# A sliding-window copy: staged batches stored as 127 rows a half instead of 128, with 15 of them on the software ring

## The chip, the cores and the metric

The kernel runs on one core of one Trainium2 chip. The metric is the device time of one execution in microseconds, the median of several; lower is better. There is no arithmetic: the kernel only moves bytes with DMAs. DMAs are issued on three queues, called rings here: SP's and ScalarE's (hardware descriptor generation; q1 and q10 in the profile) and GpSimd's (software; q0, POOL in the profile). All three feed the same 16 DMA engines.

## The reference

```python
def setup_inputs():
    batch, length, dim = (32, 4096, 256)
    window_size = 64
    stride = 32
    return {'x': np.random.randn(batch, length, dim).astype(np.float32), 'window_size': window_size, 'stride': stride}

def reference(x, window_size, stride):
    batch, length, dim = x.shape
    n_windows = (length - window_size) // stride + 1
    result = np.zeros((batch, n_windows, window_size, dim), dtype=np.float32)
    for i in range(n_windows):
        start = i * stride
        result[:, i] = x[:, start:start + window_size].copy()
    return result
```

A batch of `x` is 4096 rows of 256 float32, 4.19 MB. Cut into blocks of 32 rows it has 128 blocks of 32 KB. Window i is the blocks i and i + 1, so the 127 windows of a batch are 8.3 MB of output, in which every block but the first and the last stands twice: as the left half of window i and as the right half of window i - 1. The whole output is 266.3 MB.

## The kernel before, in words

Each batch takes one of two ways.

Twenty *direct* batches are copied from HBM to HBM. `Copier.windows` (L29, its DMA at L34) copies n windows, or n left or right halves. SP's ring copies 16 half windows (16 rows of 32 KB, 512 KB) with each DMA, 14 DMAs a batch, 280 in all (`blocks`, L166). The remaining 15 windows of a batch are one DMA of 960 KB on the software ring (`remainder`, L170); the last batch's 15 are spread over five DMAs there. That makes 24 DMAs on the software ring, all issued at the start.

Twelve *staged* batches go through SBUF on ScalarE's ring, in two groups of six tiles (`Staging`, L61). A tile `xb` has 128 rows, one block of 32 KB in each partition. `load` (L78) fills it (HBM is read once), and two half stores write it out: half 0 puts row p into the left half of window p, half 1 puts row p into the right half of window p - 1. A row is written 64 KB apart from the next, as two packets of 16 KB.

A half needs only 127 rows: row 127 is no left half, row 0 no right half. Before, all 128 rows are stored all the same, as one DMA of 128 rows or two of 64 (every other row). The row too many lands in the neighbouring batch: the left half of row 127 in window 0 of the batch after, the right half of row 0 in the last window of the batch before. So what belongs there has to be written later:

- where the neighbour is a direct batch, SP's DMA that writes that place is held back to the end (`spoilt`, L175) and waits until the staged batch is stored (`wait_stored`, L114);
- the last two staged batches are neighbours of each other; `store_pair` (L102) orders their stores, with a wait on `spilt` in the middle.

The order on each ring is written out by hand. ScalarE: six loads, twelve half stores, six loads (each waits until the tile's former batch is stored, L82), twelve half stores. GpSimd: the 24 remainders, then a drain. SP: one DMA, then three more that wait for remainders 7, 11 and 16 to land and all the rest after 17 (`back`, L192 to L198), then the held-back ones, then the waits for everything (L205).

Of the kernel before, what the change touches and what calls it, by code (L numbers as in the profile page):

```python
# [11 lines left out]
class Copier:  # L12


    def __init__(self, x, out, B, L, D, W, S, n_win):
        assert W == 2 * S and L % S == 0
        self.x, self.out = x, out
        self.B = B
        self.blk = S * D
        self.nb = L // S  # L20
        self.nw = n_win
# [18 lines left out]
    def load(self, q, t, b, c, rows):  # L40

        p, step, n, unit = rows
        return q.dma_start(
            out=t[p : p + (n - 1) * step + 1 : step, :],
            in_=self.xap(b * self.nb + c + p // unit, [[step // unit * self.blk, n], [1, self.blk]]),
            max_dma_last_dim=IN,
        )

    def store(self, q, t, b, c, rows, half):


        p, step, n, unit = rows
        w = b * self.nw + c + p // unit - half
        return q.dma_start(
            out=self.oap(2 * w + half, [[2 * step // unit * self.blk, n], [1, self.blk]]),
            in_=t[p : p + (n - 1) * step + 1 : step, :],
            max_dma_last_dim=OUT,
        )


class Staging:  # L61


    def __init__(self, c, tc, pool, dtype, items, bufs):
        self.c, self.items = c, items
        self.tiles = [pool.tile([128, c.blk], dtype, name=f"xb{i}") for i in range(bufs)]
        self.loaded = [tc.alloc_semaphore(f"loaded{i}") for i in range(bufs)]
        self.stored = [tc.alloc_semaphore(f"stored{i}") for i in range(bufs)]
        self.spilt = tc.alloc_semaphore("spilt")
        self.ended = tc.alloc_semaphore("ended")  # L70
        self.count = {sem: 0 for sem in (*self.loaded, *self.stored, self.spilt, self.ended)}
        self.after_load, self.after_store = {}, {}

    def issue(self, dma, sem):
        dma.then_inc(sem, 16)
        self.count[sem] += 16

    def load(self, q, g):  # L78
        i = g % len(self.tiles)
        b = self.items[g]  # L80
        if self.count[self.stored[i]]:
            q.wait_ge(self.stored[i], self.count[self.stored[i]])  # L82
        parts = [(k, 4, 32, 1) for k in range(4)] if g == 0 else [(0, 1, 128, 1)]
        for rows in parts:
            self.issue(self.c.load(q, self.tiles[i], b, 0, rows), self.loaded[i])
        self.after_load[g] = self.count[self.loaded[i]]

    def put(self, q, g, part, half, sem):
        k, n = part
        i = g % len(self.tiles)  # L90
        self.issue(self.c.store(q, self.tiles[i], self.items[g], 0, (k, n, 128 // n, 1), half), sem)

    def store(self, q, g):
        i = g % len(self.tiles)
        q.wait_ge(self.loaded[i], self.after_load[g])
        for half in (0, 1):
            n = 1 if (2 * g + half) % 4 == 3 else 2
            for k in range(n):
                self.put(q, g, (k, n), half, self.stored[i])
        self.after_store[g] = self.count[self.stored[i]]  # L100

    def store_pair(self, q, g):  # L102

        for k in (g, g + 1):
            q.wait_ge(self.loaded[k % len(self.tiles)], self.after_load[k])
        even, odd = (0, 2), (1, 2)
        for k, part, half in ((g, even, 1), (g, odd, 0), (g + 1, odd, 0), (g + 1, even, 1)):
            self.put(q, k, part, half, self.spilt)
        self.put(q, g, even, 0, self.ended)
        q.wait_ge(self.spilt, self.count[self.spilt])  # L110
        for k, part, half in ((g + 1, even, 0), (g, odd, 1), (g + 1, odd, 1)):
            self.put(q, k, part, half, self.ended)

    def wait_stored(self, q, g):  # L114

        if g in self.after_store:
            q.wait_ge(self.stored[g % len(self.tiles)], self.after_store[g])
        else:
            q.wait_ge(self.spilt, self.count[self.spilt])

    def run(self, q):
        bufs = len(self.tiles)
        for first in range(0, len(self.items), bufs):
            group = range(first, min(first + bufs, len(self.items)))
            for g in group:
                self.load(q, g)
            pair = group[-1] == len(self.items) - 1
            for g in group[:-2] if pair else group:
                self.store(q, g)
            if pair:  # L130
                self.store_pair(q, group[-2])


@with_exitstack
def kernel(
    ctx: ExitStack,
    tc: tile.TileContext,
    x: bass.AP,
    window_size: bass.AP,
    stride: bass.AP,  # L140
    out: bass.AP,
):
    nc = tc.nc
    W, S = int(window_size), int(stride)
    B, L, D = x.shape
    n_win = (L - W) // S + 1
    assert out.shape == (B, n_win, W, D)
    c = Copier(x, out, B, L, D, W, S, n_win)


    staged = [1, 4, 7, 10, 13, 16, 19, 22, 24, 26, B - 3, B - 2]
    place = {b: g for g, b in enumerate(staged)}
    direct = [b for b in range(B) if b not in staged]
    pool = ctx.enter_context(tc.tile_pool(name="xb", bufs=1))
    st = Staging(c, tc, pool, x.dtype, staged, 6)
    ring_d, ring_s, ring_r = nc.sync, nc.scalar, nc.gpsimd
    done = tc.alloc_semaphore("done")
    rest = tc.alloc_semaphore("rest")
    back = {i: tc.alloc_semaphore(f"back{i}") for i in (7, 11, 16, 17)}
    total = {done: 0, rest: 0, **dict.fromkeys(back.values(), 0)}  # L160

    def count(dma, sem):
        dma.then_inc(sem, 16)
        total[sem] += 16

    def blocks(part):  # L166
        for b, w, half in part:
            count(c.windows(ring_d, b, w, 16, half), done)

    def remainder(b, w, n, half=None, piece=DIRECT, sem=rest):  # L170
        count(c.windows(ring_r, b, w, n, half, piece), sem)

    first, last = 48, B - 1
    halves = [(b, w + (15 if w >= first else 0), half) for b in direct for w in range(0, 112, 16) for half in (0, 1)]
    spoilt = {(b + d, 0 if d > 0 else c.nw - 16, 0 if d > 0 else 1): g for b, g in place.items() for d in (1, -1) if b + d in direct}  # L175
    halves = [h for h in halves if h not in spoilt]
    spoilt = sorted(spoilt, key=spoilt.get)
    with tc.tile_critical():
        st.run(ring_s)

        pairs = iter([(first + d, half) for d in (0, 2) for half in (0, 1)])
        for i, b in enumerate(direct[:-1]):
            if i in (8, 9, 12, 13):
                w, half = next(pairs)
                remainder(last, w, 2, half, DIRECT // 2)
            if i == 4:
                remainder(last, first + 4, 11)
            remainder(b, first, 15, piece=DIRECT // 2 if i in (1, 3, 4, 15, 18) else DIRECT, sem=back.get(i, rest))
        ring_r.drain()  # L189

        blocks(halves[:1])
        ring_d.wait_ge(back[7], 16)  # L192
        blocks(halves[1:2])
        ring_d.wait_ge(back[11], 16)
        blocks(halves[2:3])
        ring_d.wait_ge(back[16], 16)
        blocks(halves[3:4])
        ring_d.wait_ge(back[17], 16)  # L198
        blocks(halves[4:])
        for h in spoilt:  # L200
            b = h[0] + (-1 if h[1] == 0 else 1)
            st.wait_stored(ring_d, place[b])
            blocks([h])
        total[st.ended] = st.count[st.ended]
        for sem, n in total.items():  # L205
            ring_d.wait_ge(sem, n)


# [33 lines left out]
```

## Time and profile before

| what | value |
|---|---|
| time, median of 3 runs | 748.22 us (747.45 to 749.07) |
| the profiled execution | 747.89 us |
| its span | 746.1 us |
| bytes moved by DMAs | 317.50 MB, mean 426 GB/s |
| ScalarE's ring (q10) | 151.00 MB |
| SP's ring (q1) | 146.82 MB |
| software ring (q0) | 19.66 MB |

Compute engines do nothing here but issue DMAs, so the parts of the profile on busy engines and on the chain of work say little. What carries the time is the row of DMA engines over the 40 slices of the span (digits are tenths of busy, the GB/s below), the table of queues (packets, MB, share of the sixteen engines' span), the waits of the issuing sequencers, and the list of DMA issues with the time from issue to landing. Beside these answers the trace holds a record of each packet (start, duration, size, queue; the engine is not named) and the times at which each DMA's sixteen completions landed; where a text says "the records", it is these.

### The profile page before, as it was taken

The numbers are of one execution on the slowest core, as the hardware profiler recorded it, in microseconds if no ns is written. First come the engines' busy times: TensorE is split into PE (matmuls) and PEld (weight loads), VectorE is DVE, ScalarE is ACT, GpSimd is POOL, SyncE is SP. The second block draws the span as 40 slices with busy tenths as digits, with TensorE's granted clock in tenths as the row PEclk, the third lists the DMA queues.
The fourth block names the chain that finished last, engine by engine and source line by source line (L and its number), as shares of the span: only waits on it lengthen the run. The fifth ranks groups of instructions, "written<-read, shape, count | busy, mean of one in ns | idle before, by whom it ended". The sixth has DMA issues, their size and how long they took to land. (4 is left out here: it accounts for less than half of the span.)

```text
span 746.1 us, 419 instructions
## 1 busy us (share of the span) xinstructions
POOL 14.0 (2%) x28
## 2 busy tenths in 40 slices
POOL 7000000000000000000000000000000000000000
DMA  8999999999999999999999999999999999999997
GB/s 364 433 419 430 441 416 428 428 432 429 431 432 432 434 427 433 432 432 429 432 406 432 433 432 429 432 426 433 430 428 432 433 428 431 430 432 435 430 430 326
DMA packets 20418, 317.50 MB, mean 426 GB/s; under 512 B 5962, under 2 KB 5962, under 8 KB 5962
## 3 DMA queue, kind: packets, MB, share of 16 engines
q10 hardware_dynamic: 10144, 151.00, 47.5%
q1 hardware_dynamic: 8960, 146.82, 46.0%
q0 software_dynamic: 1312, 19.66, 6.2%
q14 instruction: 2, 0.02, 0.0%
HBM read 216.79 MB, written 267.12 MB: 649 GB/s over the span
## 5 line engine op out<-in xcount | busy, mean ns | idle before, releaser
L34 POOL DMA_DIRECT2D out_dram<-in_x_dram x24 | 13.8, 577 | 1.0 <-PEq L237 1.0
L223 POOL MEMSET const-float32-0.0<- 128x1 f32 x1 | 0.1, 99 | 0.2 <-issue 0.2
L223 POOL MEMSET const-bfloat16-1.0<- 128x1 bf16 x1 | 0.1, 103 | 0.0
L223 POOL MEMSET const-float32-1.0<- 128x1 f32 x1 | 0.1, 100 | 0.0
L223 POOL MEMSET const-uint8-127<- 128x1 uint8 x1 | 0.1, 99 | 0.0
## 6 DMA issues: line engine op xcount, KB each, us to landing
out_dram<-in_x_dram SPq DMA_DIRECT2D x280, 512.0 KB, 83.4
out_dram<-xb ACTq DMA_DIRECT2D x38, 2048.0 KB, 104.4
xb<-in_x_dram ACTq DMA_DIRECT2D x11, 4096.0 KB, 121.4
out_dram<-xb ACTq DMA_DIRECT2D x5, 4096.0 KB, 113.7
out_dram<-in_x_dram POOLq DMA_DIRECT2D x19, 960.0 KB, 50.2
xb<-in_x_dram ACTq DMA_DIRECT2D x4, 1024.0 KB, 15.5
out_dram<-in_x_dram POOLq DMA_DIRECT2D x1, 704.0 KB, 23.8
out_dram<-in_x_dram POOLq DMA_DIRECT2D x4, 64.0 KB, 52.4
```

The costliest lines, as they stand in the source:

```text
L34: return q.dma_start(out=self.oap((b * self.nw + w0) * 2 + h, [[2 * blk, n], row]), in_=self.xap(b * self.nb + w0 + h, [[blk, n], row]), m ...
L223: nc = _bacc.Bacc("TRN2", target_bir_lowering=False, num_devices=1)
```

## The change

The staged halves are stored as exactly 127 rows, so nothing lands in a neighbour and nothing has to be written again.

- ScalarE's ring stores 112 rows of a half: the even rows as two DMAs of 32 (or one of 64, in every fourth half), 32 of the odd rows, and 16 more odd rows. Counted from the half's first row, these are rows 0, 4, ... and 2, 6, ... (or 0, 2, 4, ...), 1, 5, ..., and 3, 7, ..., 63.
- The software ring stores the 15 rows left, 67, 71, ..., 123 (480 KB), by `run_odd`, after its 24 remainders. POOL waits for the tile's load and for the half store before it: the left half's 15 rows for the former tile's right store, the right half's for this tile's left store.
- Semaphores are kept by tile and by kind (load, left, right, odd). A load into a used tile waits for all three kinds of stores of its former batch.
- SP's list loses the held-back DMAs: these stand at their place in the list, with no wait. It is 280 DMAs as before. At its end SP waits for the remainders, for the last six tiles' stores (`finish`) and for its own DMAs.
- `store_pair`, `wait_stored` and the `spilt` and `ended` semaphores are gone.

```diff
@@ -64,71 +64,66 @@
...
         self.tiles = [pool.tile([128, c.blk], dtype, name=f"xb{i}") for i in range(bufs)]
-        self.loaded = [tc.alloc_semaphore(f"loaded{i}") for i in range(bufs)]
-        self.stored = [tc.alloc_semaphore(f"stored{i}") for i in range(bufs)]
-        self.spilt = tc.alloc_semaphore("spilt")
-        self.ended = tc.alloc_semaphore("ended")
-        self.count = {sem: 0 for sem in (*self.loaded, *self.stored, self.spilt, self.ended)}
-        self.after_load, self.after_store = {}, {}
-
-    def issue(self, dma, sem):
+        self.sems = {k: [tc.alloc_semaphore(f"{k}{i}") for i in range(bufs)] for k in ("load", "left", "right", "odd")}
+        self.count = {sem: 0 for sems in self.sems.values() for sem in sems}
+        self.at = {("odd", g): 32 * (g // bufs + 1) for g in range(len(items))}
+
+    def issue(self, dma, kind, g):
+        sem = self.sems[kind][g % len(self.tiles)]
         dma.then_inc(sem, 16)
         self.count[sem] += 16
+        if kind != "odd":
+            self.at[kind, g] = self.count[sem]
+
+    def wait(self, q, kind, g):
+        if (kind, g) in self.at:
+            q.wait_ge(self.sems[kind][g % len(self.tiles)], self.at[kind, g])
+
+    def tile(self, g):
+        return self.tiles[g % len(self.tiles)]
 
     def load(self, q, g):
-        i = g % len(self.tiles)
-        b = self.items[g]
-        if self.count[self.stored[i]]:
-            q.wait_ge(self.stored[i], self.count[self.stored[i]])
+        for kind in ("left", "right", "odd"):
+            self.wait(q, kind, g - len(self.tiles))
         parts = [(k, 4, 32, 1) for k in range(4)] if g == 0 else [(0, 1, 128, 1)]
         for rows in parts:
-            self.issue(self.c.load(q, self.tiles[i], b, 0, rows), self.loaded[i])
-        self.after_load[g] = self.count[self.loaded[i]]
-
-    def put(self, q, g, part, half, sem):
-        k, n = part
-        i = g % len(self.tiles)
-        self.issue(self.c.store(q, self.tiles[i], self.items[g], 0, (k, n, 128 // n, 1), half), sem)
+            self.issue(self.c.load(q, self.tile(g), self.items[g], 0, rows), "load", g)
+
+    def put(self, q, kind, g, half, k, step, n):
+        self.issue(self.c.store(q, self.tile(g), self.items[g], 0, (half + k, step, n, 1), half), kind, g)
 
     def store(self, q, g):
-        i = g % len(self.tiles)
-        q.wait_ge(self.loaded[i], self.after_load[g])
-        for half in (0, 1):
-            n = 1 if (2 * g + half) % 4 == 3 else 2
-            for k in range(n):
-                self.put(q, g, (k, n), half, self.stored[i])
-        self.after_store[g] = self.count[self.stored[i]]
-
-    def store_pair(self, q, g):
-
-        for k in (g, g + 1):
-            q.wait_ge(self.loaded[k % len(self.tiles)], self.after_load[k])
-        even, odd = (0, 2), (1, 2)
-        for k, part, half in ((g, even, 1), (g, odd, 0), (g + 1, odd, 0), (g + 1, even, 1)):
-            self.put(q, k, part, half, self.spilt)
-        self.put(q, g, even, 0, self.ended)
-        q.wait_ge(self.spilt, self.count[self.spilt])
-        for k, part, half in ((g + 1, even, 0), (g, odd, 1), (g + 1, odd, 1)):
-            self.put(q, k, part, half, self.ended)
-
-    def wait_stored(self, q, g):
-
-        if g in self.after_store:
-            q.wait_ge(self.stored[g % len(self.tiles)], self.after_store[g])
-        else:
-            q.wait_ge(self.spilt, self.count[self.spilt])
+        self.wait(q, "load", g)
+        for half, kind in enumerate(("left", "right")):
+            rows = [(0, 2, 64)] if (2 * g + half) % 4 == 3 else [(0, 4, 32), (2, 4, 32)]
+            for k, step, n in (*rows, (1, 4, 32), (3, 4, 16)):
+                self.put(q, kind, g, half, k, step, n)
+
+    def odd(self, q, g, half):
+        self.wait(q, "load", g)
+        self.wait(q, *(("left", g) if half else ("right", g - 1)))
+        self.put(q, "odd", g, half, 67, 4, 15)
+
+    def groups(self):
+        n = len(self.tiles)
+        return [range(k, min(k + n, len(self.items))) for k in range(0, len(self.items), n)]
 
     def run(self, q):
-        bufs = len(self.tiles)
-        for first in range(0, len(self.items), bufs):
-            group = range(first, min(first + bufs, len(self.items)))
+        for group in self.groups():
             for g in group:
                 self.load(q, g)
-            pair = group[-1] == len(self.items) - 1
-            for g in group[:-2] if pair else group:
+            for g in group:
                 self.store(q, g)
-            if pair:
-                self.store_pair(q, group[-2])
+
+    def run_odd(self, q):
+        for g in range(len(self.items)):
+            for half in (0, 1):
+                self.odd(q, g, half)
+
+    def finish(self, q):
+        for g in self.groups()[-1]:
+            for kind in ("left", "odd", "right"):
+                self.wait(q, kind, g)
 
 
 @with_exitstack
@@ -149,7 +144,6 @@
 
 
     staged = [1, 4, 7, 10, 13, 16, 19, 22, 24, 26, B - 3, B - 2]
-    place = {b: g for g, b in enumerate(staged)}
     direct = [b for b in range(B) if b not in staged]
     pool = ctx.enter_context(tc.tile_pool(name="xb", bufs=1))
     st = Staging(c, tc, pool, x.dtype, staged, 6)
@@ -172,9 +166,6 @@
 
     first, last = 48, B - 1
     halves = [(b, w + (15 if w >= first else 0), half) for b in direct for w in range(0, 112, 16) for half in (0, 1)]
-    spoilt = {(b + d, 0 if d > 0 else c.nw - 16, 0 if d > 0 else 1): g for b, g in place.items() for d in (1, -1) if b + d in direct}
-    halves = [h for h in halves if h not in spoilt]
-    spoilt = sorted(spoilt, key=spoilt.get)
     with tc.tile_critical():
         st.run(ring_s)
 
@@ -186,6 +177,7 @@
             if i == 4:
                 remainder(last, first + 4, 11)
             remainder(b, first, 15, piece=DIRECT // 2 if i in (1, 3, 4, 15, 18) else DIRECT, sem=back.get(i, rest))
+        st.run_odd(ring_r)
         ring_r.drain()
 
         blocks(halves[:1])
@@ -197,13 +189,10 @@
         blocks(halves[3:4])
         ring_d.wait_ge(back[17], 16)
         blocks(halves[4:])
-        for h in spoilt:
-            b = h[0] + (-1 if h[1] == 0 else 1)
-            st.wait_stored(ring_d, place[b])
-            blocks([h])
-        total[st.ended] = st.count[st.ended]
-        for sem, n in total.items():
-            ring_d.wait_ge(sem, n)
+        for sem in (*back.values(), rest):
+            ring_d.wait_ge(sem, total[sem])
+        st.finish(ring_d)
+        ring_d.wait_ge(done, total[done])
 
 
 # ---- launch: one core; inputs and outputs as the reference has them ----
```

## The prediction

> **What bounds the kernel now.** I read the row of GB/s over time first, then the table of queues, the stretches of time, the waits of the DMA-issuing engines, and the DMA issues.
>
> The page's slices and its table of queues:
>
> ```profile
> DMA  8999999999999999999999999999999999999997
> GB/s 364 433 419 430 441 416 428 428 432 429 431 432 432 434 427 433 432 432 429 432 406 432 433 432 429 432 426 433 430 428 432 433 428 431 430 432 435 430 430 326
> DMA packets 20418, 317.50 MB, mean 426 GB/s; under 512 B 5962, under 2 KB 5962, under 8 KB 5962
> q10 hardware_dynamic: 10144, 151.00, 47.5%
> q1 hardware_dynamic: 8960, 146.82, 46.0%
> q0 software_dynamic: 1312, 19.66, 6.2%
> HBM read 216.79 MB, written 267.12 MB: 649 GB/s over the span
> ```
>
> q10 is ScalarE's ring (12 loads and 24 half stores of 4.19 MB each are 151.0 MB), q1 is SP's (280 x 512 KB), q0 the software ring. The three shares add up to 99.7% of sixteen engines: the time is bytes over what the engines carry. One 16 KB packet: q10 moved 9,216 of them in 0.475 x 16 x 746.1 = 5,670 us, so 0.615 us each; the packet records have 0.611 us as the median. A 32 KB packet of q1 is 0.460 x 16 x 746.1 / 4,480 = 1.226 us (median 1.213). So an engine moves 16 KB in 0.61 us, whatever ring it comes from and whether the other end is SBUF or HBM.
>
> Stretches of time (start:end, length, POOL busy, clock, DMA share, GB/s):
>
> ```profile
> 0.00:20.00 20.00, 13.96 (x28) 1.00 0.90 366
> 20.00:100.00 80.00, 0.00 (x0) 1.00 1.01 428
> 100.00:360.00 260.00, 0.00 (x0) 1.00 1.01 430
> 360.00:400.00 40.00, 0.00 (x0) 1.00 1.01 423
> 700.00:740.00 40.00, 0.00 (x0) 1.00 1.00 428
> 740.00:746.10 6.10, 0.00 (x0) 1.00 0.28 118
> ```
>
> Idle time is at the ends only: 2.0 us in the first stretch, 0.72 x 6.1 = 4.4 us in the last. In that last stretch engines finish one after another: the last landings of SP's ring spread from 742.0 to 744.8 us.
>
> Waits of SP's sequencer, and the issues (form, count, KB each, median us to landing):
>
> ```profile
> SPq L34 <- DMA out_dram<-in_x_dram: 94.4, 4, 44.3
> SPq L34 <- DMA out_dram<-xb: 48.3, 4, 40.6
> SPq L206 <- DMA out_dram<-xb: 39.8, 1, 39.8
> ```
> ```profile
> out_dram<-in_x_dram SPq DMA_DIRECT2D x280, 512.0 KB, 83.4
> out_dram<-xb ACTq DMA_DIRECT2D x38, 2048.0 KB, 104.4
> out_dram<-xb ACTq DMA_DIRECT2D x5, 4096.0 KB, 113.7
> out_dram<-in_x_dram POOLq DMA_DIRECT2D x19, 960.0 KB, 50.2
> ```
>
> The waits look long, but each ring holds 80 to 100 us of work, so a sequencer can wait 40 us and no engine runs dry. Waits cost only where a ring empties.
>
> **The change, part by part.**
>
> *Bytes.* 24 half stores of 128 rows become 127: 24 x 32 KB = 786 KB less, 48 KB an engine, three 16 KB packets: 3 x 0.611 = **-1.83 us**. Reads stay; SP's 280 DMAs stay, reordered.
>
> *Who moves them.* ScalarE's ring loses 24 x 2 = 48 packets an engine (14 for 16 a half). The software ring gains 24 DMAs of 15 rows, 30 packets each: 720/16 = 45 an engine. The difference is those three.
>
> *More DMAs.* ScalarE's stores go from 43 to 18 x 4 + 6 x 3 = 90, POOL's from 24 to 48. Each leaves a 4-byte completion packet on an engine; in the records the next packet starts 6 ns after it. 71 x 6 ns = **+0.43 us**. Issuing is covered: ScalarE's shortest issue is 0.6 us and it waits 9.1 us (median) for room in its ring; POOL's is 0.58 us and POOL has nothing else.
>
> *Evenness.* In the records the first 15-row DMA of q0 puts a 32 KB packet on fifteen engines and only a 4-byte one on the sixteenth. Read as a rotation (each DMA begins where the last one ended), the 24 old DMAs give thirteen engines 1,216 KB and three 1,088 to 1,152 KB, and tile 1's load, landing at 406.9 to 416.5 us, does show just three engines 4 to 7 us early. The 24 new ones add 736 KB to eight engines and 704 KB to the other eight. With 768 KB less on q10, that is -1.22 us on five of the thirteen that end last and -2.44 us on the other eight. Which are last at the end I can't see: three engines are 1.5 to 2.5 us late there, from slow packets. With the 0.43 us the ends are -0.8 and -2.0 us; I take the mean, **-1.4 us**, since the late ones may be of either kind.
>
> *Turns between rings.* In the steady state an engine takes one packet from each ring in turn, and a 4-byte packet uses a turn. By 100 us, 366 x 20 + 428 x 80 = 41.6 MB were moved: 19.7 of q0, 2.1 of SP's (four DMAs), so 19.8 of q10. SP then has 276 x 2 = 552 turns an engine left. ScalarE had 131.2 MB, 500 packets, and some 52 completions: 552. After: 118.6 MB, 452, and 99 completions: 551. The two rings still end together; without the smaller DMAs ScalarE's would end some 48 turns early, which would cost little, since the records show one ring alone running its packets back to back within 0.1 us. Cost 0.
>
> *Waits added.* POOL now waits for loads and for ScalarE's stores; behind it stand only further DMAs of the same kind and its drain. ScalarE's load into a used tile also waits for the two 15-row stores of it. The last such load (tile 5) went out at 375.8 us, when the right half of the store landed; its last 15-row store waits for the left half, which landed at 353.6, and needs three turns of some 2.4 us. So it has more than 10 us to spare; without them the ring still holds four loads at 18.8 us each. At the end the last 15-row store goes out when the last left half lands, some 18 turns of 1.2 us before the right one. SP's final waits are one or two more of 0.075 us. Cost 0.
>
> *Waits removed.* SP's 48.3 us of waiting for staged stores and ScalarE's wait inside its last pair go. Both rings were full meanwhile (1.00 busy from 700 to 740 us). Gain 0.
>
> *Fewer partitions.* The 16-row and 15-row stores touch one half of SBUF. The nearest row is tile 0's load, 32 rows four apart: its four DMAs landed 9.8, 14.6, 20.1 and 24.6 us in, 4.5 to 5.5 us for eight packets (half q0's), which is 8 x 0.611 = 4.9. I take 0. The other end, half speed for all these packets, is 93 x 0.611 = 57 us; nothing points to it.
>
> *Sum:* -1.83 + 0.43 = -1.4 us. The profiled execution took 747.89 us (span 746.1 and 1.8 around it) and would take 746.5; it lies 0.33 us under the median of the three runs, so in medians 748.22 - 1.4 = **746.8 us**.
>
> [...]
>
> **Rivals.**
>
> 1. *Slower: each late arrival on the software ring stalls the engines.* Until now q0 works only before 105 us; then it comes up 24 times alone in the steady state. Speaks for it: slow packets gather where the mix changes (96 to 102 us, when SP's ring comes in, lost 0.3 us an engine; 372 to 380 us, from stores to loads, 0.85). Against: between 20 and 100 us, with q0 always at work, 428 GB/s. Priced by the first, 24 x 0.3 = +7.2 us: 754.0; by the four slices of 20 us in which q0 worked, which lost 0.6 us together, +0.6: 747.4. Over 0.06 us an arrival it takes the gain. It is slower than before by my bound from 0.12 us; middle 750.
>
> 2. *No change: the 15 rows always fall on the same fifteen engines.* Then those gain 24 x 32 = 768 KB on q0 for 768 KB lost on q10, and only the completions are left: 748.65. Against it: the second old DMA again leaves out one engine, but not the same one. [...]
>
> 3. *Faster: the end gets more even.* The last stretch loses 4.4 us an engine on average. If SP's order behind the staged stores has a part in it, up to 2 us more go: 744.8. Against: both rings were full, and the spread is as old as 43 us.
>
> [...]
>
> **How the numbers follow.** Forecast 0.59, rival 1 0.21, rival 2 0.08, rival 3 0.10, rival 4 0.02. I call 0.2%, 1.5 us, about what can be told from no change. The forecast's own range is 746.0 to 747.5; with the 0.8 us by which runs differ, 0.33 of its 0.59 fall beyond 1.5 us faster, 0.26 within. Faster: 0.33 + 0.10 = 0.43. Same: 0.26, less than half of rival 2 and a little of rival 1: 0.30. Slower: 0.27, the remainder of the rivals. The range goes down to rival 3 and up past the middle of rival 1: 744.8 to 751.0; left out is the upper part of rivals 1 and 4.
>
> **What would show it.** q10 138.42 MB in 10,128 packets, q1 unchanged, q0 31.46 MB, 266.34 MB written; 430 GB/s in the slices up to 740 us. Rotation: SP's last landings spread by no more than before. Rival 1: slices of 400 to 425 GB/s after 100 us, with longer packets. Wrong turns: one ring's last landing many us before the other's. I would be wrong if an engine ran dry in the middle, or if stores from half the partitions took over 0.7 us a packet.

## The result, and the profile after

The changed kernel takes 767.25 us (median of 5 runs, 764.73 to 767.83), the kernel before 748.34 us beside it: a ratio of 1.0247, 95% interval 1.0228 to 1.0266. It is 18.9 us slower. The forecast was 1.4 us faster, and the range ended at 751.0 us, so both the sign and the range were wrong.

The page of the kernel after, its slices and its queues (packets, MB, share of sixteen engines):

```profile
GB/s 363 426 432 430 426 428 430 424 420 420 417 426 422 412 420 419 420 426 418 428 420 424 430 428 430 430 431 430 426 420 425 421 419 420 412 421 417 426 390 128
q1 hardware_dynamic: 8960, 146.82, 45.3%
q10 hardware_dynamic: 10128, 138.42, 42.8%
q0 software_dynamic: 2464, 31.46, 10.3%
HBM read 216.79 MB, written 266.34 MB: 631 GB/s over the span
```

The bytes are what the change says, to the last digit: 138.42 MB in 10,128 packets on ScalarE's ring, 31.46 MB on the software ring, 266.34 MB written. What changed is the rate. Half way through the span there are slices of 428 to 431 (ScalarE loads its second six tiles); on both sides of them, where it stores, nearly all slices are at 412 to 426. The same by stretches of time (start:end, length, POOL busy, clock, DMA share, GB/s):

```profile
110.00:290.00 180.00, 3.87 (x7) 1.00 1.01 421
400.00:500.00 100.00, 0.55 (x1) 1.00 1.00 428
500.00:700.00 200.00, 4.97 (x9) 1.00 1.01 422
740.00:765.50 25.50, 0.55 (x1) 1.00 0.44 179
```

Two of these stretches in the kernel before:

```profile
110.00:290.00 180.00, 0.00 (x0) 1.00 1.01 431
500.00:700.00 200.00, 0.00 (x0) 1.00 1.01 431
```

There are two losses. First, in the store stretches the engines are as busy as ever (1.01) and carry 2% less: nothing runs dry, the packets take longer. The shares of the queues say how much: 98.4% of 765.5 us is 753.3 us of packet time an engine, against 99.7% of 746.1 = 743.9 us before, for fewer bytes: 9.4 us. Second, the end: 0.56 x 25.5 = 14.3 us an engine are idle in the last stretch, against 4.4 before; the last sixteen completions on SP's ring come in from 757.3 to 764.0 us, while some engines finished near 747 (by the records sixteen packets are under way at 740 us, four at 758). So the longer packets do not fall on all engines alike, and the last one ends the kernel. 9.4 + 9.9 = 19.3 is the difference of the two spans (19.4).

Which packets? In the records, after 110 us, a 16 KB packet of the software ring takes 0.724 us on average, up to 2.48; the old ones took 0.615. On the other rings, 16 KB takes 0.619 (0.613 before) and 32 KB 1.228 (1.216). The 690 late packets of the software ring are few, but they are the ones that lengthened most. Counted over 0.611 us for 16 KB and 1.213 us for 32 KB, an engine loses 5.2 us on the software ring's packets (0.2 before), 4.5 on SP's (1.3) and 4.5 on ScalarE's (2.1): about half of what was added falls on the other two rings.

POOL's waits, by the trace:

```profile
POOL out_dram L54 <- DMA out_dram<-xb: 665.0, 22, 124.0
POOL out_dram L54 <- DMA xb<-in_x_dram: 50.0, 2, 39.2
```

POOL sits in its new waits nearly all the time, and that costs nothing: behind them are only its own further stores. ScalarE waited 1.2 us for a store before its last load, with the ring full of other loads.

### The profile page after: what moved, and what is told of

Its sections match the earlier page's. It is cut to its first block, busy times and chain, and to the rows that moved or that the text cites. A ratio compares the mean times of both kernels' runs of the same rounds, so it can differ in the third digit from the quotient of the medians.

```text
span 765.5 us, 527 instructions
## 1 busy us (share of the span) xinstructions
POOL 27.2 (4%) x52
## 3 DMA queue, kind: packets, MB, share of 16 engines
q10 hardware_dynamic: 10128, 138.42, 42.8%
q0 software_dynamic: 2464, 31.46, 10.3%
HBM read 216.79 MB, written 266.34 MB: 631 GB/s over the span
## 4 chain that ended last, share of the span: by engine, by line
another core or an unknown queue 90%; DMA 3%; issue 2%; POOL 2%; ACTq 0%; POOLq 0%; SPq 0%
DMA xb<-in_x_dram 3%; POOL out_dram L54 2%; ACTq L43 0%; POOLq L181 0%; POOLq L80 0%; ACTq L226 0%; SPq L169 0%
## 5 line engine op out<-in xcount | busy, mean ns | idle before, releaser
L54 POOL DMA_DIRECT2D out_dram<-xb x24 | 13.3, 553 | 715.0 <-DMA out_dram<-xb 665.0
```

Source lines behind the costliest of these rows:

```text
L54: return q.dma_start(out=self.oap(2 * w + half, [[2 * step // unit * self.blk, n], [1, self.blk]]), in_=t[p : p + (n - 1) * step + 1 : ste ...
```

## The experiments

Three theories stood at the start. A: the software ring's late arrivals, one at a time, stall engines (rival 1 of the prediction). B: reading few partitions of SBUF with many engines makes packets slow (the part I had priced at 0). C: the smaller DMAs on ScalarE's ring. The chips differ by up to 3.5 us in the time of the kernel before, so each set has its own.

### Three ways to take the change apart, and one to make it worse

The 15-row stores read from HBM:

```diff
-        self.put(q, "odd", g, half, 67, 4, 15)
+        self.issue(self.c.again(q, self.items[g], half + 67, 4, 15, half), "odd", g)   # again(): the same rows, out of x in HBM
```

> The changed kernel, but the 24 late 15-row stores of the software ring read their rows from x in HBM instead of the tile in SBUF; sizes, order, waits and destinations are the same. Theory A (the late arrival on the software ring is what stalls engines, whatever it reads): 764 to 768 us, slow packets around each arrival as before, slices near 420 GB/s. Theory B (reading SBUF in that form, fifteen engines at one half of the partitions, is what makes packets slow): 746 to 750 us, slices of 430. Theory C (the smaller DMAs on ScalarE's ring are the cause): 764 to 768 us, with the slow packets on ScalarE's ring.

The 15-row stores on ScalarE's ring:

```diff
+            self.put(q, "odd", g, half, 67, 4, 15)   # in store(), behind the half's other stores
-        st.run_odd(ring_r)
```

> The changed kernel, but the 15-row stores go on ScalarE's own ring, behind the other stores of their half; the software ring has only its 24 old DMAs. Theory A: 747 to 752 us, the software ring being idle late (the ring of ScalarE has 48 more data turns and would end last, alone). Theory B: 760 us or more, since the same rows are read by as many engines. Theory C: 764 us or more.

The kernel before with small stores:

```diff
+        tail = [(1, 4, 32), (3, 4, 16), (67, 4, 16)]
+        pieces = {(0, 2): [(0, 4, 32), (2, 4, 32)], (1, 2): tail, (0, 1): [(0, 2, 64), *tail]}[part]
```

> The kernel before, with all 128 rows on ScalarE's ring, but cut as the change cuts them: 64 or 32 + 32 even rows, 32 odd rows, and 16 + 16 odd rows. Theory C: slower than before by most of the 19 us. Theories A and B: 747 to 751 us, the completions alone (about 75 more an engine, 0.5 us) and an end that is a little less even.

Rows in blocks:

```diff
-            for k, step, n in (*rows, (1, 4, 32), (3, 4, 16)):
+            rows = [(0, 1, 64)] if (2 * g + half) % 4 == 3 else [(0, 1, 32), (32, 1, 32)]
+            for k, step, n in (*rows, (64, 1, 32), (96, 1, 16)):
-        self.put(q, "odd", g, half, 67, 4, 15)
+        self.put(q, "odd", g, half, 112, 1, 15)
```

> The changed kernel with the same DMA sizes on the same rings, but rows in blocks: ScalarE's ring stores rows 0 to 63, 64 to 95, 96 to 111 of a half, the software ring the 15 rows 112 to 126. Theory A: 764 to 768 us as before. Theory B: a different time, slower than 768 us if engines that read neighbouring partitions get in each other's way, since fifteen engines then read fifteen neighbouring partitions. Theory C, if the stride is the point: faster.

Measured, the kernel before at 744.87 us:

| run | us | against before (95%) |
|---|---|---|
| 15 rows from HBM | 754.78 | 1.0135 (1.0118 to 1.0152) |
| 15 rows on ScalarE's ring | 757.97 | 1.0166 (1.0146 to 1.0186) |
| before, small stores | 754.58 | 1.0129 (1.0114 to 1.0144) |
| rows in blocks | 805.9 and 820.7 | two runs |

None of the three theories came out whole. Reading HBM instead of SBUF left 9.9 us where the changed kernel loses 19 to 22. The last run is the loudest: no DMA's size, ring or place in the order was touched, only which rows go together, and it cost some 40 us more than the change. That points to the partitions, and to neighbours as the worse ones (the rows in HBM move with them, so it shows no more than that). But small stores alone, with no late arrival at all, cost 9.7 us as well. Part of that is the end: there ScalarE's ring had more turns than SP's. SP's last packet ended at 735.6 us, ScalarE's ran on to 751, and the stretches say that engines that nearly all read SBUF do worse:

```profile
110.00:290.00 180.00, 0.00 (x0) 1.00 1.01 427
400.00:500.00 100.00, 0.00 (x0) 1.00 1.01 430
500.00:700.00 200.00, 0.00 (x0) 1.00 1.01 428
720.00:740.00 20.00, 0.00 (x0) 1.00 0.98 390
```

With the 15-row stores on ScalarE's ring, SP's last packet ended at 717.2 us, and 720 to 740 us ran at 320 GB/s (share 0.94). The times of that run and of this one are therefore not clean measures of the stores themselves; the stretches before 700 us are. Small stores alone show 427 and 428 there, against 431. The 15-row stores on ScalarE's ring:

```profile
110.00:290.00 180.00, 0.00 (x0) 1.00 1.01 429
500.00:700.00 200.00, 0.00 (x0) 1.00 1.01 429
```

These are the same rows, read from the same partitions 67 to 123, as in the changed kernel with its 421 and 422 (421 and 419 on a chip as fast as this one, below). In these two stretches a 16 KB packet of ScalarE's ring, the 15 rows among them, takes 0.614 us on average. So these partitions alone do not make packets slow; it takes the software ring to read them. No run separates why: a third ring reading SBUF beside ScalarE's, or another division of the rows among the engines. With 757.97 us the run lies between the range of theory A and those of B and C.

### Arrivals, partitions, and the stores left out

The changed kernel once more; without the 15-row stores (`run_odd` not called, its waits dropped); the 15 rows from HBM, all issued at once with no wait; and this, which only changes the source:

```diff
-        self.put(q, "odd", g, half, 67, 4, 15)
+        w = self.items[g] * self.c.nw + 67
+        self.issue(q.dma_start(
+            out=self.c.oap(2 * w + half, [[8 * self.c.blk, 15], [1, self.c.blk]]),
+            in_=self.tile(g)[half + 35 : half + 92 : 4, :],
+            max_dma_last_dim=OUT,
+        ), "odd", g)
```

> The changed kernel again, on the chip of the runs beside it: 18 to 20 us over the kernel before.

> The changed kernel without its 24 stores of 15 rows (15 rows of every staged half are not written, 11.8 MB less). At 0.611 us a packet this is 45 packets an engine or 27.5 us less than the 1.4 us under the kernel before that I forecast: 28.9 us under it, if ScalarE's 64-, 32- and 16-row stores cost nothing. What is missing from 28.9 is the price of those stores (theory C): the slices of the run before with small stores, 427 and 428 GB/s against 431, give about 3 us, so 25 to 27 us under. If theory C had most of the loss: 10 to 20 us under.

> The changed kernel, but the 24 stores of 15 rows read from x in HBM and are issued in one go behind the 24 old DMAs of the software ring, with no wait: the software ring is at work until about 190 us and then idle. Against the run where they come one by one (9.9 us over the kernel before). Theory A (coming one at a time stalls engines): 2 to 4 us over the kernel before, what is left being ScalarE's small stores. If it is not the arrivals but the stores themselves (512 KB apart in HBM, fifteen engines): 8 to 11 us over.

> The changed kernel, but the 15-row stores read partitions 35, 39 to 91 (36 to 92 for the right half) instead of 67 to 123, so that the fifteen partitions lie in both halves of SBUF; destinations, sizes, waits and order are the same (what these 15 rows hold is then another block's data). Theory B in the form that engines reading partitions 32 apart share a way out of SBUF: 754 to 758 us, as with the rows from HBM, on a chip where the kernel before takes 745. If only the number of partitions counts, or reading SBUF from the software ring at all: 763 to 767 us.

Measured, the kernel before at 745.09 us:

| run | us | against before (95%) |
|---|---|---|
| changed kernel | 767.46 | 1.0297 (1.0263 to 1.0331) |
| without the 15-row stores | 719.25 | 0.9652 (0.9638 to 0.9666) |
| 15 rows from HBM, at once | 754.09 | 1.0119 (1.0102 to 1.0136) |
| 15 rows from partitions 35 to 91 | 751.58 | 1.0087 (1.0067 to 1.0108) |

The last row is the answer to most of it. Reading other partitions, with everything else as it was, takes 15.9 us of the 22.4 away, and the time is under even the 754 to 758 us expected. (The changed kernel lost 22.4 us on this chip where 18 to 20 were expected.) The stretches of the changed kernel on this chip, and of the run with the rows spread:

```profile
110.00:290.00 180.00, 3.87 (x7) 1.00 1.01 421
400.00:500.00 100.00, 0.55 (x1) 1.00 1.01 431
500.00:700.00 200.00, 4.42 (x8) 1.00 1.01 419
```

```profile
110.00:290.00 180.00, 3.87 (x7) 1.00 1.01 428
400.00:500.00 100.00, 0.00 (x0) 1.00 1.00 429
500.00:700.00 200.00, 4.97 (x9) 1.00 1.01 428
```

POOL issues the same stores at the same points, and 419 to 421 become 428. The late 16 KB packet of the software ring falls from 0.727 to 0.644 us in the mean, and those over 0.7 us from 124 to 37 of 690.

Theory A falls with the third row: coming all at once or one by one, rows from HBM cost 9.0 and 9.9 us. Their loss only moves. Issued at once, it is all between 110 and 290 us:

```profile
110.00:290.00 180.00, 0.00 (x0) 1.00 1.01 412
400.00:500.00 100.00, 0.00 (x0) 1.00 1.01 431
500.00:700.00 200.00, 0.00 (x0) 1.00 1.01 431
```

Why rows from HBM cost that much is not shown. (The expectation calls them 512 KB apart in HBM; in the edit they are read 128 KB apart and written 256 KB apart.)

Without the 15-row stores the kernel is 25.8 us under the one before. Bytes and completions give 1.83 + 27.5 - 0.28 = 29.0, so the 64-, 32- and 16-row stores cost 3.2 us on this chip.

### How many partitions, and how far apart

Two questions: is it that a DMA stays in one half of SBUF, or something finer; and does a complete kernel made by the answer win? In the first of these runs the 15 rows are divided so that no two partitions of one DMA are 32 apart within one half of SBUF:

```diff
-            for k, step, n in (*rows, (1, 4, 32), (3, 4, 16)):
+            for k, step, n in (*rows, (1, 4, 32), (35, 4, 16)):
-        self.put(q, "odd", g, half, 67, 4, 15)
+        self.put(q, "odd", g, half, 3, 4, 8)
+        self.put(q, "odd", g, half, 99, 4, 7)
```

> A complete version made by theory B: of the rows 3, 7 to 123 of a half, ScalarE's ring stores the 16 from 35 to 95, and the software ring the other 15 as a DMA of 8 rows (3 to 31) and one of 7 (99 to 123), issued together. In each of these DMAs no two rows are 32 apart in the same half of SBUF. Theory B: the gain of the run with the 15 rows spread holds, and the 16-row stores get cheaper too: 744 to 751 us where the kernel before takes 745; under 744 it beats both. If the spread had helped there only because half of the rows lie in the lower half: 755 us or more.

> The changed kernel, but the 15-row stores read fifteen neighbouring partitions (112 to 126, 113 to 127), destinations and all else unchanged (these rows then hold other blocks' data). [...] From 751.6 (one) and 767.5 us (two), some 16 us a further engine: 790 to 815 us. If neighbours do not matter: 764 to 770 us.

In the third, ScalarE's 16 rows are `(3, 8, 16)` and the software ring's 15 are `7, 8, 15`:

> The changed kernel with the rows 3, 7 to 123 divided the other way: ScalarE's 16 are 3, 11 to 123, the software ring's 15 are 7, 15 to 119. Both lie in both halves of SBUF, but still with pairs of rows 32 apart in the same half. Theory B (32 apart is what counts): 762 to 770 us, as the changed kernel. If it is enough that both halves are used: 750 to 756 us.

Measured, the kernel before at 747.92 us, and beside them what the records say of the late 16 KB packets of the software ring (mean, and how many of 690 took over 0.7 us):

| 15 rows read from | us | against before (95%) | mean us | over 0.7 us |
|---|---|---|---|---|
| 112 to 126, neighbours | 798.61 | 1.0692 (1.0632 to 1.0753) | 1.355 | 406 |
| 7, 15 to 119 | 768.2 | 1.026 (1.0233 to 1.0287) | 0.744 | 136 |
| 67, 71 to 123 (the change) | 767.46 | 1.0297 (1.0263 to 1.0331) | 0.727 | 124 |
| 3 to 31 and 99 to 123 | 755.49 | 1.0102 (1.0087 to 1.0117) | 0.645 | 53 |
| 35, 39 to 91 | 751.58 | 1.0087 (1.0067 to 1.0108) | 0.644 | 37 |

(The third and fifth are of the set above, on another chip.) Using both halves is not enough: every eighth row does, and is as slow as the change. The stretches of the run with neighbours:

```profile
110.00:290.00 180.00, 3.87 (x7) 1.00 1.01 401
400.00:500.00 100.00, 0.55 (x1) 1.00 1.00 427
500.00:700.00 200.00, 3.86 (x7) 1.00 1.01 401
```

The table goes by how far the partitions of a DMA are apart. From 7 to 119 and from 67 to 123 there are pairs 32 apart within one half of SBUF (7 and 39, 67 and 99): 0.744 and 0.727 us a packet. In the last two rows there is no such pair: 0.645 and 0.644. Neighbours take 1.355. This is measured on the software ring alone; on ScalarE's ring, above, 67 to 123 were not slow (429 GB/s). What two such partitions share is not shown. The 790 to 815 us expected of the neighbours are added up from 751.6 us for one engine and 767.5 for two, with some 16 us for each further one. No run shows such a count, since no record names an engine or a partition; 798.61 us was measured.

The complete kernel among these, with rows 3 to 31 and 99 to 123, is some 11 us better than the change, on ratios of 1.0102 and 1.0247, but it does not beat the kernel before: it is 7.6 us slower, between its two ranges.

### What is left

Two rests were open: the 3 us of the small stores, and the 5 us that spread 15-row stores still cost over their bytes (719.25 + 27.6 is 746.9, and 751.6 was measured). In the run without 15-row stores, and in the run with them spread, the 16-row stores were made to read 35 to 95 as well (their rows then hold other blocks' data). And two complete kernels without small reads of SBUF were tried:

```diff
+            self.put(q, kind, g, half, 0, 1, 112)      # one store a half; or two, of 16 KB a row each
+        for b in staged:
+            for half in (0, 1):
+                remainder(b, 112, 15, half, DIRECT // 2)   # 15 windows from HBM, software ring
```

> The run without the 15-row stores (25.8 us under the kernel before), with ScalarE's 16-row stores reading partitions 35 to 95 (36 to 96), no two 32 apart in one half, instead of 3 to 63; destinations and all else unchanged (these rows then hold other blocks' data, and 15 rows of every staged half are not written). If the 3 us that the small stores cost are the 16-row stores' partitions: 28 to 29 us under the kernel before. If they are the number or the size of the DMAs, or the end: 25 to 26.5 us under.

> The run with the 15-row stores reading partitions 35 to 91 (6.5 us over the kernel before), with the 16-row stores reading 35 to 95 as well. If the rest is the 16-row stores' partitions: 2 to 4 us over. If what is left is that the software ring's engines read SBUF while ScalarE's do, out of step with them: 6 to 8 us over.

> A complete version without small reads of SBUF: ScalarE's ring stores rows 0 to 111 of a half (1 to 112) as two DMAs of 112 rows, the first and the second 16 KB of each row, seven neighbouring partitions an engine; the 15 windows 112 to 126 of a half are copied from HBM to HBM by the software ring, 24 DMAs of 480 KB issued behind its 24 old ones, with no wait. It moves the same bytes as the changed kernel. If partitions read by few engines at a time were the whole loss, this gives the forecast: 1 to 2 us under the kernel before (0.998). If 112 rows seven to an engine collide too, or fifteen rows from HBM cost as in the run where they were issued early (9 us over): 5 us over or more.

> The same with one DMA of 112 rows for each half. ScalarE's ring then has 24 completions an engine fewer and gets its turns done earlier, some 67 turns before SP's, which then runs alone for about 40 us. One ring of HBM to HBM alone ran back to back in the records: within 1 us of the other. If SP alone is slower: up to 4 us over it.

Measured, the kernel before at 747.73 us: 726.55 without 15-row stores and the 16 spread (0.9719, 0.9706 to 0.9731); 751.87 with both spread (1.0056, 1.0042 to 1.007); 777.09 and 804.03 for the two complete ones (1.0383, 1.0358 to 1.0408, and 1.0749, 1.0704 to 1.0794).

With both spread the kernel is 4.1 us over the one before (3.1 to 5.2 by the interval), at the upper end of the first range and outside the second. But the parts do not add up here as on the other chip. The 15-row stores cost 751.87 - 726.55 = 25.3 us, 2.3 less than their bytes and completions, and the store stretches run at 428 GB/s with them, at 426 and 421 without. So the rest of 5 us that was to be explained is not there on this chip, and what the cut stores cost depends on what else runs.

The last two are plain misses: 29 and 56 us slower. All their stores have 112 rows or come from HBM in the form that SP's have, and yet the stretch from 500 to 680 us, long after the software ring is done, runs at 405 GB/s with one store of 112 rows (its late 16 KB packets of ScalarE's ring take 0.665 us, 745 of them over 0.7). These 112 rows have pairs 32 apart in both halves, but so have the 128- and 64-row stores of the kernel before, which ran at 431 GB/s. So such pairs in one DMA are not the whole answer. A guess is that what matters is which engine reads which partitions, seven neighbours each instead of eight. The records don't name the engine, and it wasn't tried.

Nor are the 29 and 56 us the price of these stores alone. ScalarE's ring was done before SP's, and SP's copies, nearly alone, were slow too. With one store a half, beside the stretch named above:

```profile
500.00:680.00 180.00, 0.00 (x0) 1.00 1.00 405
740.00:758.00 18.00, 0.00 (x0) 1.00 1.01 352
```

In the second stretch 177 of 210 data packets are SP's, and 32 KB take 1.49 us on average in place of 1.22. The expectation of that run had a ring of HBM to HBM copies alone running back to back. Why SP's copies are slower there is not shown.

The first was 21.2 us under the kernel before where the run on another chip had 25.8, with the 16 rows better spread. So the three forms of the 16-row store went on one chip:

> The changed kernel without the 15-row stores once more (15 rows of every staged half not written), 16-row stores from partitions 3 to 63, for the two beside it: 24 to 27 us under the kernel before.

> The same with the 16-row stores reading partitions 35 to 95. If the other chip made it worse: as the run beside it or better, 25 to 29 us under the kernel before. If the partitions did: 20 to 23 us under.

> The same with the 16-row stores taking rows 3, 11 to 123 (4, 12 to 124): if a DMA gives each engine a run of its rows, engine e reads partition 8e + 3, inside the eight partitions that it reads in the 128-, 64- and 32-row stores too. If what costs is an engine leaving its own eight partitions: 28 to 29 us under the kernel before, the best of the three. If only pairs 32 apart count (there are such pairs here): as the first of the three.

Measured, the kernel before at 748.04 us (15 rows of every staged half are not written in any of them; in the second the 16 rows hold other data):

| 16-row stores read | us | against before (95%) |
|---|---|---|
| 3 to 63 | 728.64 | 0.9743 (0.9727 to 0.976) |
| 35 to 95 | 727.25 | 0.9729 (0.9714 to 0.9743) |
| 3, 11 to 123 | 729.13 | 0.9755 (0.9739 to 0.9772) |

It goes with the chip: the same kernel that lost 3.2 us on the other lost 9.6 here (29.0 less 19.4, where 24 to 27 were expected for the 19.4). The second form, 20.8 us under, falls into the range that was to speak for its partitions, but the first, without them, is slower still. The partitions of the 16-row stores move it by 1 to 2 us at most, the intervals overlap, and no form is at 29. The stretches of the first of the three:

```profile
110.00:290.00 180.00, 0.00 (x0) 1.00 1.01 423
400.00:500.00 100.00, 0.00 (x0) 1.00 1.01 431
500.00:700.00 200.00, 0.00 (x0) 1.00 1.01 423
```

So without the 15-row stores ScalarE's 64-, 32- and 16-row stores cost 3 to 10 us, by the chip, in the stretches where they run (7.8 on the chip of the set before, 29.0 less 21.2). Their slow packets are many small ones (397 on its own ring and 541 on SP's took more than 0.06 us longer than usual), SP's too, which read no SBUF at all. What lengthens them is open: it is not the partitions of the 16-row stores, and the runs don't separate the number of DMAs from the order in which rows reach HBM.

## Why the prediction was wrong

By its own steps:

- *Bytes, who moves them, number of DMAs:* right to the packet, as the queues show.
- *Fewer partitions: "I take 0".* This is the step that failed, and it gave the wrong sign. The 15-row stores lose 20.6 us over their bytes (767.46 - 719.25 = 48.2, less 27.6 for bytes and completions), and 15.9 of these go when they read other partitions. The sign of being wrong that I had named, over 0.7 us a packet, came true with 0.724. For stores on ScalarE's ring 0 was about right: other partitions move the 16-row stores by 1 to 2 us, and the 15 rows on that ring left 429 GB/s. The row that I took as nearest, tile 0's load of 32 rows, goes over partitions 0 to 127, on ScalarE's ring, and writes SBUF; the new stores read it, 67 to 123 on the software ring (0.727 us a packet there, and 0.644 from 35 to 91). I named the other end, 57 us, said that nothing points to it, and left it out of the range. The row differs from the new stores in ring, direction and partitions, so it should have stayed a bound.
- *More DMAs: 0.43 us.* This term was too small. The completions are small (9 ns each in the records), but ScalarE's cut stores cost 3.2 us on one chip and 9.6 on another. The forecast priced a completion and a turn and no other effect on neighbouring packets.
- *Evenness: -0.8 to -2.0 us.* The rotation was not what counted. Slow packets fell on some engines more than on others (eight packets are under way at 747 us, four at 758) and left 14.3 us idle at the end instead of 4.4.
- *Turns between rings:* right where it was undisturbed; from 500 to 700 us the records have 2,775 packets of SP's ring and 2,770 of ScalarE's in the kernel before (2,746 and 2,745 in the changed one), the 4-byte ones counted, and all sixteen engines are busy until 736 us. The runs that broke the balance showed that I was wrong in thinking a ring alone costs nothing: with SBUF stores nearly alone the engines ran at 390 and 320 GB/s, with SP's copies nearly alone at 352.
- *Waits added and removed: 0.* Right. POOL's 715 us of waiting cost nothing, and SP's former 48 us gained nothing. (Loads land some 20 us apart, where I had 18.8 a load; nothing hung on that.)
- *Rival 1* had sign and place (slices of 412 to 426 after 100 us, longer packets on the software ring), and the wrong mechanism: rows from HBM that come at once cost as much as one by one. Its 754.0 us was also far too low.
- *Small DMAs that leave gaps, 0.02 as rival 4:* they left none, as forecast (the DMA share is 1.01 in the stretches where they run), but cutting the stores was not free: 3 to 10 us for 47 more DMAs on ScalarE's ring.
- *Rivals 2 and 3* end at 748.65 and 744.8 us and can't give the loss.

The sum, on the one chip that had all the parts: -1.4 as forecast, +3.2 for the cut stores (29.0 expected, 25.8 measured), +15.9 for the partitions of the 15-row stores, +4.7 for these stores even when spread: +22.4, which is 767.46 - 745.09 by construction. The last 4.7 are not explained, and on the chip where both stores were spread they were not there (25.3 us for the 15-row stores, against 27.6), so the sum holds for its own chip.

## What to carry to other kernels

When DMAs fill all engines, a change that moves fewer bytes can still lose by making packets longer (here 0.8 MB less, and 421 GB/s in place of 431 at a DMA share of 1.01): look at the GB/s of stretches where the DMA share is 1.00 and at the packets' durations, and don't take a busy share for a rate. Before cutting a store into pieces, look at which partitions each DMA reads, and which ring reads them: the same 15 rows left 429 GB/s on ScalarE's ring and 421 on the software ring. The 690 late packets of the software ring took 0.727 us each from one set of partitions and 0.644 from another; with nothing else changed that was 15.9 us, and the bytes that the change saved were worth 1.83. And a price of zero needs a row with the same access pattern; where there is none, its other end belongs in the range.

## What the runs showed of the hardware that was not expected

- Only the source partitions of 3.7% of the bytes, read by the software ring, decide between 751.6 and 767.5 us, and on another chip 798.6: no pair 32 apart within a half, such pairs, and neighbours.
- A kernel with one DMA of 112 rows a half, and the other rows from HBM, is 56 us slower than the one with 128 rows, and with the same rows in two halves of each row 29 us; an uneven end has a part in it.
- One ring nearly alone ran slower in three stretches than two in turn (431 GB/s): at 390 and 320 with stores out of SBUF, at 352 with copies from HBM to HBM.
- The kernel before varies by 3.5 us between chips (744.9 to 748.3), and a kernel with cut stores by 9 (719.25 and 728.64).
